# Seven-product tiles of an up product: four weight pieces, three interleaved tiles, other times for the weight sums

## The chip, the cores and the metric

One core of a Trainium2 chip runs one whole encoder layer. The metric is the device time of one execution in microseconds (us), as the median of several runs; lower is better. The engines are PE (TensorE, the matmuls), DVE (VectorE), ACT (ScalarE), POOL (GpSimd) and SP (SyncE, which here only issues DMAs). Each engine works through its own instructions in order and waits on semaphores for the others.

## The reference

The input is one sequence of 512 positions with 1024 features, float32. The layer has a mixing half (retention, and a gated unit that mixes over positions) and a feed-forward half. What the change touches is the first product of the feed-forward half:

```python
def _conv_gated_mlp(h, w_up, conv_w, conv_b, w_down):
    hid = h @ w_up                                   # (512, 1024) @ (1024, 5632)
    ...
    hid = lax.conv_general_dilated(                  # over 3 neighbouring positions, channel by channel
        ...) + conv_b
    a, b = jnp.split(hid, 2, axis=-1)
    return (jax.nn.gelu(a) * b) @ w_down             # (512, 2816) @ (2816, 1024)

# in reference()
h = _rmsnorm(x, g_pre_mix)
proj = h @ w_in                                      # q, k, v, g, u, sv and two gates
...
x = x + _rmsnorm(merged @ w_out, g_post_mix)
h2 = _rmsnorm(x, g_pre_ffn)
x = x + _rmsnorm(_conv_gated_mlp(h2, w_up, conv_w, conv_b, w_down), g_post_ffn)
```

## The kernel before

A float32 product is made as three matmuls of a faster type: each operand is split into a high and a low part, and hi·hi, hi·lo and lo·hi are added in PSUM. `split` makes the parts of a weight block: ACT copies it to `wf` or `wh` (the high part, by `copy`, L105), DVE subtracts that from the raw block (L163).

**Stages.** In the profile the projections and the retention lie up to about 215 us, u and the two gates from 215 to 400, the output projection, the norms and the first tiles of the up product up to about 480, the rest of the up product to about 650, the down product after that.

**The up product.** It makes 22 tiles of 128 channels of a and of b. Twelve of them, three in each of four groups (GROUPS, the first tile numbers 4, 8, 12, 16), are made with seven half-size products instead of eight (class `Pair`, after Strassen and Winograd); the fourth tile of a group is made whole, as two blocks of 24 matmuls of 128x512 (`f_block`). The three are called a, b and c below. A product of a Pair is twelve matmuls of 128x256. Its products, in the order in which one tile takes them, are M1 and M1' (`part1`, with the weight as it is), S1, S2, S3 (with sums of the activations and of the weights), and the two of `part3`, x4 and S4. M1 and S2, S3 and x4 gather in one PSUM bank: M1 is copied out by ACT first, then S2 is added to the bank and copied out again, and so on. So S2 waits for M1's copy. Where a tile's seven products lie between those of the others is written out by hand, in the loop over `i`.

**The weights of a Pair.** Blocks are fetched in the order of the list `units`, ahead of their use (`w_get`): SP issues the load into a raw buffer (`raw_tile`, four buffers), then the block is split. A seven-product tile has the unit u1 (the weight, 1024 columns), u2 (two sums, t12, 1024 columns), u3 (a third sum, 512) and u4 (a fourth sum and the rest of the weight, 1024).

**The weight sums.** The sums t12, t3 and t4 of a tile are not made by an engine but by DMAs from the weights in DRAM into DRAM: a copy (`sums_copy`, issued by ACT) and accumulating transfers (`sums_add`, issued by POOL, L131), seven for each tile. SUMS_AT says at which count of calls of `copy` each is issued, so it sets when they run. In the profiled execution count 67 falls at 133 us, 104 at 170, 140 at 213, 150 at 226, 285 at 396, 312 at 483 and 360 at 555.

**After the products.** `tile_done` convolves a finished tile (`conv`: steps on ACT L1321 and DVE L1324, L1328), applies gelu (ACT L1335), multiplies (DVE, `gp`, L1337) and, at the tiles of FORMS_AT, makes the forms of the activations for the down product (`down_forms`): sums `fs` and differences on DVE (L1363 to L1366), each high part `fh` by ACT's copy, and for the low part `fl` ACT writes −fh (L1346) and POOL issues an accumulating DMA that adds the source (L1347). `tc.issue_after(x)` holds what is within it back behind instruction x.

**Buffers.** `blk` gives blocks of 512 columns from one pool of 66 that many values share (c, gp, fs, fh, fl); who gets which is settled in the order of the program. The scheduler then orders the instructions of each engine by its own estimate of times.

Of the kernel before, what the change touches and what calls it, by code (L numbers as in the profile page):

```python
# [17 lines left out]
S = 512  # L18
# [24 lines left out]
).split()]  # L43
GROUPS = range(4, 20, 4)
SEVENS = [i + n for i in GROUPS for n in range(3)]
SUMS_AT = [a + k * (b - a) // n for a, b, n in ((29, 67, 28), (106, 140, 14), (150, 285, 14), (286, 300, 7), (312, 360, 21)) for k in range(n)]
FORMS_AT = (7, 9, 11, 13, 17, 19, 20, 21)

PRE, FFNG, LNG, LNB = 0, 8, 16, 24
# [6 lines left out]
def tile_block(ctx: ExitStack, tc, xT, x, wall, par, cs, wsp, bsp, gpost, gffn, out):  # L56
# [11 lines left out]
    def blk(dt=F32, n="blk", shape=(P, S)):  # L68
        return sb.tile(list(shape), dt, tag="blk", bufs=NBLK, name=nm(n))
# [34 lines left out]
    def copy(o, i):  # L104
        done = nc.scalar.activation(out=o, in_=i, func=AF.Copy)  # L105
        copies[0] += 1
        while sums_at and copies[0] >= sums_at[0]:
            sums_at.pop(0)
            sums_ops.pop(0)(done.ins)
        return done  # L110
# [35 lines left out]
    def two(t):  # L146
        return t.rearrange("p (n c) -> p n c", n=2)
# [13 lines left out]
    def split(hi, lo, src):  # L161
        copy(hi, src)
        low[0] = nc.vector.tensor_sub(lo, src, as32(hi)).ins  # L163
# [3 lines left out]
    RES1 = NW - 22 - 44  # L167
    RES0 = RES1 - RES_OUT
    FORMS = ("B11", "B21", "T1", "T2", "T3", "T4", "B22")
    units = []  # L170
    i = 0
    while i < NW:
        pair = [(f, i) for f in FORMS]
        if i == SV0:
            units += [(f, k) for f in ("s11", "sT1", "sT2") for k in range(2)]
            units += [(f, k) for k in range(2) for f in ("s22", "sT3")]
            units += [(f, k) for f in ("s21", "sT4") for k in range(2)]
            i = U0
        elif i == U0:
            us, gs = ([[(f, k + n * m) for f in FORMS] for n in range(KD // 2)] for k, m in ((U0, 2), (GATE0, 4)))  # L180
            ws = [("blk", GATE0 + 4 * (n // 2) + 2 + n % 2) for n in range(KD)]
            for what, n in MIDDLE:
                units += {"W": lambda: ws[n : n + 1], "U1": lambda: us[n][:4], "U2": lambda: us[n][4:],
                          "G1": lambda: gs[n][:4], "G2": lambda: gs[n][4:]}.get(what, list)()
            i = GATE0 + 2 * KD
        elif GATE0 <= i < GATE1:
            units += pair[:4] + [("blk", i + 2)] + pair[4:] + [("blk", i + 3)]
            i += 4
        elif i == UP0 + 2 * GROUPS[0]:
            for g in GROUPS:  # L190
                a, b, c = ([(f, g + n) for f in ("u1", "u2", "u3", "u4")] for n in range(3))
                w = [("blk", UP0 + 2 * (g + 3) + n) for n in range(2)]
                units += a[:2] + b[:2] + a[2:3] + w[:1] + a[3:] + b[2:3] + c[:2] + b[3:] + c[2:3] + w[1:] + c[3:]
            i = UP0 + 2 * (GROUPS[-1] + 4)
        elif i == DOWN0:
            for _ in range(2):
                pairs = [[("q", i + j), ("t", i + j)] for j in range(DP)]
                whole = [[("blk", i + DP)], [("blk", i + DP + 1)]]
                for u in pairs[:4] + whole[:1] + pairs[4:6] + whole[1:] + pairs[6:] if i == DOWN0 else pairs + whole:
                    units += u  # L200
                i += DP + WHOLE // 2
        else:
            units.append(("blk", i))
            i += 1
# [3 lines left out]
    def raw_tile():  # L208
        return sb.tile([P, 1024], F32, tag="raw", bufs=4, name=nm("raw"))
# [4 lines left out]
    def slot(n, at=0, w=1024):  # L214
        return sb.tile([P, 1088], F32R, tag="w4", bufs=9, name=nm(n))[:, at : at + w]
# [46 lines left out]
    def w_up(form, i):  # L262

        t12, t3, t4 = sums[SEVENS.index(i)]
        raw, i = raw_tile(), UP0 + 2 * i
        if form == "u3":
            raw = raw[:, :S]
            nc.sync.dma_start(raw, t3)
            w = slot("wf", 0, 1088)
            lo, hi = w[:, AT_64 : AT_64 + S], w[:, S + AT_192 : 2 * S + AT_192]  # L270
        else:
            if form == "u4":
                nc.sync.dma_start(raw[:, :S], t4)
                nc.sync.dma_start(raw[:, S:], wall[i + 1, :, S:])
            else:
                nc.sync.dma_start(raw, wall[i] if form == "u1" else t12)
            hi, lo = slot("wf", AT_192), slot("wf", AT_64)
        split(hi, lo, raw)
        return hi, lo

# [64 lines left out]
    kinds = {"b": lambda _, i: w_block(i), "u": w_up, "q": w_down, "t": w_down, "s": w_sv}  # L345

    def w_size(u):
        return 2 if u[0] in ("blk", "q", "t", "u1", "u2", "u4") or u[0][0] == "s" else 1

    def w_get(look=LOOK):  # L350

# [623 lines left out]
    class Pair:  # L975
# [39 lines left out]
        def part1(self):  # L1015

            c0, c1 = self.t

            def second():
                o = self.product(1, self.x(4, T0), True)  # L1020
                self.sum = v.tensor_add(two(c0[:, T0]), o, two(c0[:, T0])).ins

            o = self.product(0, self.x(0, T0), True)
            copy(two(c0[:, T0]), o)
            second()
            self.product(2, self.s("S1"), True)
            o = self.product(0, self.s("S2"), False)
            self.copied = copy(two(c1[:, T0]), o).ins
            if self.scale is not None:
                v.tensor_mul(c0[:, T0], c0[:, T0], self.scale[:, T0])  # L1030
# [9 lines left out]
        def part3(self):  # L1040
            c0, c1 = self.t
            o = self.product(0, self.x(4, T1), False, self.w[0])
            if self.scale is None:
                copy(two(c0[:, T1]), o)
            else:
                v.tensor_mul(two(c0[:, T1]), o, two(self.scale[:, T1]))
                if self.func:
                    nc.scalar.activation(out=c0, in_=c0, func=self.func)
            o = self.product(2, self.s("S4"), False, self.w[1])
            v.tensor_sub(two(c1[:, T0]), o, two(c1[:, T0]))  # L1050
            if self.scale is not None:
                v.tensor_mul(c1, c1, self.scale)
                if self.func:
                    nc.scalar.activation(out=c1, in_=c1, func=self.func)
# [264 lines left out]
    def conv(o, m):  # L1319
        c = tmp("cv")  # L1320
        nc.scalar.activation(  # L1321
            out=c, in_=o, func=AF.Identity, scale=col(CW + 3 * m + 1), bias=col(CB + m)
        )
        v.scalar_tensor_tensor(  # L1324
            out=c[:, 1:S], in0=o[:, 0 : S - 1], scalar=col(CW + 3 * m), in1=c[:, 1:S],
            op0=ALU.mult, op1=ALU.add,
        )
        v.scalar_tensor_tensor(  # L1328
            out=c[:, 0 : S - 1], in0=o[:, 1:S], scalar=col(CW + 3 * m + 2), in1=c[:, 0 : S - 1],
            op0=ALU.mult, op1=ALU.add,  # L1330
        )
        return c

    def gated(ca, cb):
        nc.scalar.activation(out=ca, in_=ca, func=AF.Gelu_apprx_tanh)  # L1335
        gp.append(blk(n="gp") if len(gp) < 2 * DP else (hi192, lo64)[len(gp) % 2]("gp", F32))
        v.tensor_mul(gp[-1], ca, cb)  # L1337
# [43 lines left out]
        dforms.append(forms_)  # L1381

    def tile_done(i, o):
        gated(*(conv(t, 2 * i + s_) for s_, t in enumerate(o)))
        if i in FORMS_AT:
            down_forms(len(dforms))

# [10 lines left out]
            split(h_, l_, s_)  # L1398
            h2forms[n] += [(h_[:, t], l_[:, t]) for t in (T0, T1)]

    def seven(alloc=tmp):
        p = Pair(None, lambda: alloc(n="c"), (h2h, h2l, h2forms))
        p.part1()
        return p

    i, waiting = 0, []
    while i < NF:
        if i in GROUPS:
            a = seven()
            with tc.issue_after(a.copied):  # L1410
                while waiting:
                    tile_done(*waiting.pop(0))
            b = seven(blk)
            a.part2()
            o = [f_block(h2h, h2l, KD)]
            a.part3()
            b.part2()
            c = seven(blk)
            with tc.issue_after(c.copied):
                tile_done(i, a.t)  # L1420
            b.part3()
            c.part2()
            with tc.issue_after(c.copied):
                tile_done(i + 1, b.t)
            o.append(f_block(h2h, h2l, KD, c.part3))
            waiting += [(i + 2, c.t), (i + 3, o)]
            i += 4
        else:
            o = []
            for e in (2 * i, 2 * i + 1):  # L1430
                o.append(early_o[e] if e < EARLY else f_block(h2h, h2l, KD))
                while waiting:
                    tile_done(*waiting.pop(0))
            tile_done(i, o)
            for k in {0: (0,), 1: (2,)}.get(i, ()):
                h2_forms(k)
            i += 1
# [319 lines left out]
```

## Time and profile before

| | |
|---|---|
| median of 3 runs (lowest, highest) | 792.87 us (792.85, 793.17) |
| the profiled execution | 793.08 us, of which the span is 791.3 |
| granted TensorE clock | 0.998 |
| PE busy | 774.7 us, 98% of the span |
| DVE, ACT, POOL busy | 630.4, 490.8, 145.6 us |
| HBM read and written | 125.94 and 29.36 MB |

The span runs from the first instruction to the last; 1.8 us of the time lie outside it. Busy times are read against the span. A line of the profile names a group by its line in the kernel, the engine, and output<-inputs by tile names; L105 and L163 are the helpers `copy` and `split`, so one reads those by their tiles (c<-ps is a copy out of PSUM, fh<-fs a form, wf<-raw a weight).

### The profile page before, as it was taken

The page shows a single profiled execution, that of the slowest core. Times are in us where ns is not written, and L with a number is a line of the kernel's source. Part 1 is how long each engine was busy: PE and PEld are TensorE (multiplying, and loading weights), DVE is VectorE, ACT ScalarE, POOL GpSimd, SP SyncE. Part 2 cuts the span into 40 slices and gives each one's busy share as a digit, 9 for nine tenths or more (in the row PEclk, how much of TensorE's full clock was granted, in tenths as well). Part 3 has the DMA queues.
Part 4 walks back from the last instruction along what each step waited for, and adds up shares of the span by engine and source line. Part 5 has one row for each costly group of instructions (what it writes and reads, how often), then busy time and mean ns, then how long its engine had stood idle before and what let it go on. Part 6 is the DMA issues. An engine that isn't in the chain of part 4 may idle for free. (4 is left out here: it accounts for less than half of the span.)

```text
span 791.3 us, 13995 instructions
## 1 busy us (share of the span) xinstructions
PE 774.7 (98%) x5283; PEld 722.2 (91%) x5283; DVE 630.4 (80%) x1057; ACT 490.8 (62%) x878; POOL 145.6 (18%) x180
## 2 busy tenths in 40 slices
PE   9999999999999999999999999999999999999996
PEld 8888998998999999899998898999889998999996
DVE  6477887889788997977764669778787979987887
ACT  7555468788475764744553676466778767854532
POOL 0040231232212201242230211011321102300001
PEclk9999999999999999999999999999999999999999
DMA  8796798467734443445469216797977764853344
GB/s 284 266 277 189 173 224 256 105 164 176 207 97 130 108 142 116 129 123 143 165 209 353 86 55 168 244 252 198 247 195 215 188 198 92 167 168 108 107 160 160
DMA packets 51827, 139.43 MB, mean 176 GB/s; under 512 B 6320, under 2 KB 8240, under 8 KB 51568
## 3 DMA queue, kind: packets, MB, share of 16 engines
q1 hardware_dynamic: 33120, 97.25, 37.0%
q0 software_dynamic: 13936, 27.53, 19.3%
q10 hardware_dynamic: 4704, 13.77, 5.2%
q8 instruction: 41, 0.67, 0.4%
q14 instruction: 26, 0.21, 0.1%
HBM read 125.94 MB, written 29.36 MB: 196 GB/s over the span
## 5 line engine op out<-in xcount | busy, mean ns | idle before, releaser
L105 ACT ACTIVATE wf<-raw 128x512 fp32r<-128x512 f32 (+1 forms) x132 | 97.0, 743 | 92.4 <-DMA raw<-wall 29.1
L999 PE MATMUL ps<-sh,wf 128*128 128x256 f32 x768 | 141.6, 277 | 5.2 <-ACT c L105 2.2
L163 DVE TENSOR_TENSOR wf<-raw,wf 128x512 fp32r<-128x512 f32 (+1 forms) x132 | 120.9, 923 | 29.2 <-ACT wf L105 28.6
L999 PEld LDWEIGHTS ps<-sh,wf 128*128 128x128 f32 x768 | 122.0, 192 | 8.5 <-ACT c L105 3.4
L163 DVE TENSOR_TENSOR wl<-raw,wh 128x1024 fp32r<-128x1024 f32 (+1 forms) x76 | 88.1, 1169 | 47.2 <-ACT wh L105 16.3
L999 PE MATMUL ps<-sl,wf 128*128 128x256 f32 x384 | 105.5, 275 | 0.0
L105 ACT ACTIVATE wh<-raw 128x1024 fp32r<-128x1024 f32 (+2 forms) x80 | 76.7, 970 | 30.9 <-DMA raw<-wall 19.7
L999 PEld LDWEIGHTS ps<-sl,wf 128*128 128x128 f32 x384 | 73.7, 192 | 0.2
L367 PE MATMUL ps<-h2l,wh 128*128 128x512 f32 (+1 forms) x192 | 66.3, 345 | 0.4 <-DVE h2l L1257 0.3
L366 PE MATMUL ps<-h2h,wh 128*128 128x512 f32 (+1 forms) x192 | 66.3, 345 | 0.0
L368 PE MATMUL ps<-h2h,wl 128*128 128x512 f32 (+1 forms) x192 | 66.1, 344 | 0.0
L1460 PE MATMUL ps<-dl,fh 128*128 128x256 f32 x216 | 59.5, 275 | 0.9 <-DVE dl L163 0.9
L1460 PE MATMUL ps<-dh,fh 128*128 128x256 f32 x216 | 59.4, 275 | 0.0
L1460 PE MATMUL ps<-dh,fl 128*128 128x256 f32 x216 | 59.4, 275 | 0.0
L999 PE MATMUL ps<-xh,wf 128*128 128x256 f32 x288 | 52.2, 275 | 0.8 <-ACT sig L105 0.8
L999 PE MATMUL ps<-h2h,wf 128*128 128x256 f32 x288 | 52.4, 275 | 0.0
L105 ACT ACTIVATE dh<-raw 128x768 fp32r<-128x768 f32 (+1 forms) x36 | 33.5, 947 | 26.4 <-DVE raw L295 18.8
L700 PE MATMUL ps<-wh,xh 128*128 128x512 f32 x128 | 48.6, 380 | 0.0
L701 PE MATMUL ps<-wl,xh 128*128 128x512 f32 x128 | 48.5, 379 | 0.0
L702 PE MATMUL ps<-wh,xl 128*128 128x512 f32 x128 | 48.4, 379 | 0.0
L999 PEld LDWEIGHTS ps<-xh,wf 128*128 128x128 f32 x288 | 45.6, 192 | 1.2 <-ACT sig L105 0.9
L999 PEld LDWEIGHTS ps<-h2h,wf 128*128 128x128 f32 x288 | 45.7, 192 | 0.5 <-ACT c L105 0.2
(345 smaller groups left out, 2223.1 us busy)
## 6 DMA issues: line engine op xcount, KB each, us to landing
raw<-wall SPq DMA_DIRECT2D x132, 512.0 KB, 4.5
x<-x SPq DMA_DIRECT2D x24, 256.0 KB, 5.9
sum<-wall ACTq DMA_DIRECT2D x12, 512.0 KB, 6.4
sum<-wall ACTq DMA_DIRECT2D x24, 256.0 KB, 6.0
sum<-wall POOLq DMA_DIRECT2D x24, 256.0 KB, 6.2
sum<-sum POOLq DMA_DIRECT2D x24, 256.0 KB, 6.2
raw<-sum SPq DMA_DIRECT2D x12, 512.0 KB, 6.2
raw<-sum SPq DMA_DIRECT2D x24, 256.0 KB, 3.6
```

The costliest lines, as they stand in the source:

```text
L105: done = nc.scalar.activation(out=o, in_=i, func=AF.Copy)
L163: low[0] = nc.vector.tensor_sub(lo, src, as32(hi)).ins
L366: nc.tensor.matmul(o, ah, bh, start=start, stop=False, skip_group_check=skip)
L367: nc.tensor.matmul(o, ah, bl, start=False, stop=False, skip_group_check=skip)
L368: pe_last[0] = nc.tensor.matmul(o, al, bh, start=False, stop=stop, skip_group_check=skip).ins
L700: nc.tensor.matmul(acc[t], xh[k][:, c], turns(wh[:, f]), start=k == 0, stop=False)
L701: nc.tensor.matmul(acc[t], xh[k][:, c], turns(wl[:, f]), start=False, stop=False)
L702: part_end[0] = nc.tensor.matmul(acc[t], xl[k][:, c], turns(wh[:, f]), start=False, stop=k == KD - 1)
L999: self.last = nc.tensor.matmul(o, w_[:, c], a_, start=first and k == n == 0, stop=k == 3 and n == 2, skip_group_check=True,)
L1460: nc.tensor.matmul(o, a_[:, c], turns(w_[:, f]), start=j == t == i == 0, stop=j == DP - 1 and i == 2 and n not in (M2, M3, M4), skip_group ...
```

## The change

A seven-product tile gets its weight in other pieces: uB (the weight, 1024 columns, a raw buffer), u1 and u2 (the two halves of t12) and u3, 512 columns each, in `ur` buffers that come from `blk`, and u4 as before. A group thus has 8 loads into raw buffers instead of 14, and 9 into `ur`, and one split more for each tile. `part1` ends after S1; S2 is a part of its own. The three tiles are interleaved in another way, and the end of c is put into the next group, behind the first products of its a. The result buffers of all three tiles now come from `blk`; those of a did not before. And the sums' times change: none is issued between count 140 and 312; 15 more come before it, 6 more after.

```diff
-SUMS_AT = [a + k * (b - a) // n for a, b, n in ((29, 67, 28), (106, 140, 14), (150, 285, 14), (286, 300, 7), (312, 360, 21)) for k in range(n)]
+SUMS_AT = [a + k * (b - a) // n for a, b, n in ((25, 67, 32), (68, 104, 10), (106, 140, 15), (312, 366, 27)) for k in range(n)]
...
-                a, b, c = ([(f, g + n) for f in ("u1", "u2", "u3", "u4")] for n in range(3))
+                a, b, c = ([(f, g + n) for f in ("uB", "u1", "u2", "u3", "u4")] for n in range(3))
                 w = [("blk", UP0 + 2 * (g + 3) + n) for n in range(2)]
-                units += a[:2] + b[:2] + a[2:3] + w[:1] + a[3:] + b[2:3] + c[:2] + b[3:] + c[2:3] + w[1:] + c[3:]
+                units += a[:2] + last + b[:2] + a[2:3] + b[2:3] + w[:1] + a[3:4] + b[3:4]
+                units += c[:2] + a[4:] + b[4:] + c[2:3] + w[1:] + c[3:4]
+                last = c[4:]
...
     def w_up(form, i):
...
+        if form in ("uB", "u4"):
+            raw = raw_tile()
...
+        else:
+            raw = blk(n="ur")
+            nc.sync.dma_start(raw, {"u1": t12[:, :S], "u2": t12[:, S:], "u3": t3}[form])
+            w = slot("wf", 0, 1088)
...
         if i in GROUPS:
             a = seven()
-            with tc.issue_after(a.copied):
-                while waiting:
-                    tile_done(*waiting.pop(0))
-            b = seven(blk)
+            while waiting:
+                waiting.pop(0)(a.first)
+            b = seven()
+            a.part_s2()
+            b.part_s2()
+            o = [f_block(h2h, h2l, KD)]
+            with tc.issue_after(b.copied):
+                o.append(conv(o[0], 2 * i + 6))
             a.part2()
-            o = [f_block(h2h, h2l, KD)]
+            b.part2()
+            c = seven()
             a.part3()
-            b.part2()
-            c = seven(blk)
-            with tc.issue_after(c.copied):
+            b.part3()
+            with tc.issue_after(b.ended):
                 tile_done(i, a.t)
-            b.part3()
-            c.part2()
+            c.part_s2()
             with tc.issue_after(c.copied):
                 tile_done(i + 1, b.t)
-            o.append(f_block(h2h, h2l, KD, c.part3))
-            waiting += [(i + 2, c.t), (i + 3, o)]
+            o.append(f_block(h2h, h2l, KD))
+            c.part2()
+
+            def rest(after, i=i, c=c, o=o):
+                with tc.issue_after(after):
+                    c.part3()
+                    tile_done(i + 2, c.t)
+                    tile_done(i + 3, [o[0], o[1], conv(o[2], 2 * i + 7)])
+
+            waiting.append(rest)
```

`a.first` is the copy of M1, `b.ended` that of x4. In the order that the scheduler gives PE, a group now runs: M1, M1', S1 of a; x4, S4 of the c before it; M1, M1', S1 of b; S2 of a; a whole block and S2 of b (in groups 2 and 3 the block first); S3 of a, of b; M1, M1', S1 of c; x4, S4 of a, of b; S2 of c; the second block; S3 of c.

The first place is ACT's queue in group 3, where the copy of b's M1 stands. In before, c_6684 with ps_6686 is the copy of tile b's M1, c_6572 with ps_6574 belongs to tile a, fh and fl are the down product's forms:

```order
L105 ACTIVATE fh_6669<-fs_6664 128x512 [waits DVE_49]
L105 ACTIVATE c_6572<-ps_6574 128x256 [waits PE_49]
L1346 ACTIVATE fl_6670<-fh_6669 128x512 [waits Activation_49]
L105 ACTIVATE fh_6674<-gp_5976 128x512
L105 ACTIVATE wf_6806<-raw_6803 128x1024 [waits DMAHW7_49,DMAHW6_49,PE_49]
L1346 ACTIVATE fl_6675<-fh_6674 128x512 [waits Activation_49]
L105 ACTIVATE fh_6679<-gp_5911 128x512 [waits DVE_49]
L1346 ACTIVATE fl_6680<-fh_6679 128x512 [waits Activation_49]
L105 ACTIVATE c_6684<-ps_6686 128x256 [waits DMASW3_49]
```

In the changed kernel the same forms; c_6703 with ps_6705 is the copy of tile b's M1, the two c that follow are the copies of S2 of a and of b:

```order
L1332 ACTIVATE cv_6673<-ps_6528,part 128x512
L105 ACTIVATE fa_6680<-gp_5942 128x256
L105 ACTIVATE fh_6688<-fs_6683 128x512 [waits DVE_49]
L1357 ACTIVATE fl_6689<-fh_6688 128x512 [waits DMASW0_49,Activation_49]
L105 ACTIVATE fh_6693<-gp_5974 128x512
L1357 ACTIVATE fl_6694<-fh_6693 128x512 [waits Activation_49]
L105 ACTIVATE fh_6698<-gp_5942 128x512 [waits DVE_49]
L1357 ACTIVATE fl_6699<-fh_6698 128x512 [waits Activation_49]
L105 ACTIVATE c_6703<-ps_6705 128x256 [waits DMASW5_49,DMASW4_49,PE_49]
L105 ACTIVATE c_6573<-ps_6574 128x256 [waits PE_49]
```

The copy of b's M1 stands behind all six forms in both; the weight split and the copy for tile a that lay among the forms have moved out of them.

DVE's queue of the changed kernel ahead of those forms begins when c_6336, of the tile c before, has had its S4 added (L1061):

```order
L1061 TENSOR_TENSOR c_6336<-ps_6339,c_6336 128x256 [waits PE_49]
L163 TENSOR_TENSOR wf_6555<-ur_6553,wf_6555 128x512 [waits DMAHW2_49,Activation_49]
L1335 SCALAR_TENSOR_TENSOR cv_6662<-c_6335,part,cv_6662 128x511 [waits Activation_49]
L163 TENSOR_TENSOR wf_6579<-ur_6577,wf_6579 128x512 [waits DMAHW3_49,Activation_49]
L163 TENSOR_TENSOR wf_6584<-ur_6582,wf_6584 128x512 [waits DMAHW4_49,Activation_49]
L1339 SCALAR_TENSOR_TENSOR cv_6662<-c_6335,part,cv_6662 128x511 [waits DVE_49]
L163 TENSOR_TENSOR wl_6628<-raw_6625,wh_6627 128x1024 [waits Activation_49]
L163 TENSOR_TENSOR wf_6633<-ur_6631,wf_6633 128x512 [waits DMAHW5_49,Activation_49]
```

Four more convolution steps, two gp and the sums for the forms follow these rows; the four splits of 512 columns now lie between the steps.

The second place is SP's queue of loads for group 4. Before, tile 16's first pieces (sum_0_90 is its t12) and tile 17's (sum_0_93) go to raw buffers:

```order
L276 DMA raw_6967<-sum_0_90 128x1024 [waits DMASW6_49,DMAHW0_49,DMASW2_49,DVE_49]
L276 DMA raw_7021<-wall 128x1024 [waits DMAHW1_49,DVE_49]
L276 DMA raw_7040<-sum_0_93 128x1024 [waits DMAHW2_49,DMASW5_49,DMAHW3_49,DMASW1_49,DVE_49]
L268 DMA raw_7089<-sum_1_91 128x512 [waits DMAHW4_49,DMASW0_49,DVE_49]
L221 DMA raw_7120<-wall 128x1024 [waits DMAHW5_49,DVE_49,Activation_49]
```

In the changed kernel:

```order
L273 DMA raw_7325<-sum_2_95 128x512 [waits DMAHW4_49,DMASW0_49,DMAHW7_49,DVE_49,Activation_49]
L274 DMA raw_7325<-wall 128x512
L280 DMA ur_7077<-sum_0_93 128x512 [waits DMASW5_49,Activation_49]
L280 DMA ur_7101<-sum_0_90 128x512 [waits DMASW2_49,DVE_49,Activation_49]
L280 DMA ur_7106<-sum_0_93 128x512 [waits DMASW4_49,DMAHW0_49,DMASW3_49,Activation_49]
L280 DMA ur_7155<-sum_1_91 128x512 [waits DMAHW6_49,DMAHW1_49,DVE_49]
L225 DMA raw_7370<-wall 128x1024 [waits DMAHW2_49,DVE_49]
```

ur_7101 (u2 of tile 16) has the buffer of `fs_7026`, and its load waits for the DMA of POOL that reads it (fl_7032<-fs_7026); ur_7106 (u2 of tile 17) waits in the same way for fl_7037<-gp_6136. The u4 load of tile 17 (raw_7325) now stands ahead of all of these.

More of the change, by code (lines that the diff above doesn't have):

```diff
@@ L169, in tile_block @@
     FORMS = ("B11", "B21", "T1", "T2", "T3", "T4", "B22")
-    units = []
+    units, last = [], []
     i = 0
@@ L190, in tile_block @@
             for g in GROUPS:
-                a, b, c = ([(f, g + n) for f in ("u1", "u2", "u3", "u4")] for n in range(3))
+                a, b, c = ([(f, g + n) for f in ("uB", "u1", "u2", "u3", "u4")] for n in range(3))
                 w = [("blk", UP0 + 2 * (g + 3) + n) for n in range(2)]
-                units += a[:2] + b[:2] + a[2:3] + w[:1] + a[3:] + b[2:3] + c[:2] + b[3:] + c[2:3] + w[1:] + c[3:]
+                units += a[:2] + last + b[:2] + a[2:3] + b[2:3] + w[:1] + a[3:4] + b[3:4]
+                units += c[:2] + a[4:] + b[4:] + c[2:3] + w[1:] + c[3:4]
+                last = c[4:]
             i = UP0 + 2 * (GROUPS[-1] + 4)
+            units += [("blk", i)] + last
+            i += 1
         elif i == DOWN0:
@@ L264, in w_up @@
         t12, t3, t4 = sums[SEVENS.index(i)]
[L265 to L271, printed above, removed]
+        i = UP0 + 2 * i
+        if form in ("uB", "u4"):
+            raw = raw_tile()
             if form == "u4":
@@ L275, in w_up @@
             else:
-                nc.sync.dma_start(raw, wall[i] if form == "u1" else t12)
+                nc.sync.dma_start(raw, wall[i])
             hi, lo = slot("wf", AT_192), slot("wf", AT_64)
+        else:
+            raw = blk(n="ur")
+            nc.sync.dma_start(raw, {"u1": t12[:, :S], "u2": t12[:, S:], "u3": t3}[form])
+            w = slot("wf", 0, 1088)
+            lo, hi = w[:, AT_64 : AT_64 + S], w[:, S + AT_192 : 2 * S + AT_192]
         split(hi, lo, raw)
@@ L347, in w_size @@
     def w_size(u):
-        return 2 if u[0] in ("blk", "q", "t", "u1", "u2", "u4") or u[0][0] == "s" else 1
+        return 2 if u[0] in ("blk", "q", "t", "uB", "u4") or u[0][0] == "s" else 1
     def w_get(look=LOOK):
@@ L1023, in part1, with part_s2 @@
             o = self.product(0, self.x(0, T0), True)
-            copy(two(c0[:, T0]), o)
+            self.first = copy(two(c0[:, T0]), o).ins
             second()
             self.product(2, self.s("S1"), True)
+            if self.h is xh:
+                self.part_s2()
+        def part_s2(self):
+            c0, c1 = self.t
             o = self.product(0, self.s("S2"), False)
@@ L1043, in part3 @@
             if self.scale is None:
-                copy(two(c0[:, T1]), o)
+                self.ended = copy(two(c0[:, T1]), o).ins
             else:
@@ L1383, in tile_done @@
     def tile_done(i, o):
-        gated(*(conv(t, 2 * i + s_) for s_, t in enumerate(o)))
+        if len(o) == 2:
+            o = [conv(t, 2 * i + n) for n, t in enumerate(o)]
+        gated(*o[-2:])
         if i in FORMS_AT:
@@ L1399, in h2_forms, with seven @@
             h2forms[n] += [(h_[:, t], l_[:, t]) for t in (T0, T1)]
-    def seven(alloc=tmp):
-        p = Pair(None, lambda: alloc(n="c"), (h2h, h2l, h2forms))
+    def seven():
+        p = Pair(None, lambda: blk(n="c"), (h2h, h2l, h2forms))
         p.part1()
@@ L1432, in tile_block @@
                 while waiting:
-                    tile_done(*waiting.pop(0))
+                    waiting.pop(0)(pe_last[0])
             tile_done(i, o)
```

## The prediction

> **What bounds the kernel now.** First the head of the page and the waits of PE over the whole span (engine and line, what it waited for, total us, times, longest):
>
> ```profile
> span 791.3 us, 13995 instructions
> PE 774.7 (98%) x5283; PEld 722.2 (91%) x5283; DVE 630.4 (80%) x1057; ACT 490.8 (62%) x878; POOL 145.6 (18%) x180
> ...
> PE ps L999 <- ACT sig L105: 2.8, 4, 0.9
> PE ps L999 <- ACT c L105: 2.2, 4, 0.9
> ...
> PE ps L999 <- DVE c L1036: 0.5, 1, 0.5
> ```
>
> TensorE sets the time: it is idle for 791.3 − 774.7 = 16.6 us in all, and the change leaves its matmuls as many as they were. So the change is worth what it does to PE's waits. Next the stretches, with PE, PEld, DVE, ACT and POOL busy, the granted clock, the share of the DMA engines and GB/s; the rows are the retention, u and the gates, and then two of the up product:
>
> ```profile
> 40.00:215.00 175.00, 175.00 (x977) 157.45 (x977) 140.24 (x244) 115.92 (x202) 45.55 (x65) 1.00 0.75 196
> 215.00:400.00 185.00, 181.74 (x1320) 171.68 (x1319) 155.22 (x245) 109.35 (x186) 42.27 (x33) 1.00 0.46 133
> ...
> 520.00:560.00 40.00, 39.81 (x307) 37.99 (x306) 31.76 (x48) 28.57 (x49) 10.61 (x13) 1.00 0.89 224
> 560.00:600.00 40.00, 37.61 (x285) 35.44 (x283) 33.32 (x51) 29.60 (x53) 6.97 (x8) 1.00 0.79 213
> ```
>
> PE never waits beside the retention, 3.3 us beside u and the gates, 2.7 us in the up product (the two rows of the waits for c), nearly all of it from 560 to 600. The clock is 1.00 throughout. The timeline of PE (start, duration) shows what a wait there is, and how long a piece of work is. Of eight such places the first is the row at 553.17, the last the row at 602.18:
>
> ```profile
> 553.17 0.38 PE L999 MATMUL ps<-sh,wf 128*128 128x256 f32 x1
> ...
> 588.55 0.38 PE L366 MATMUL ps<-h2h,wh 128*128 128x512 f32 x1
> ...
> 593.74 0.27 PE L999 MATMUL ps<-h2h,wf 128*128 128x256 f32 x1
> ...
> 596.41 0.28 PE L999 MATMUL ps<-h2h,wf 128*128 128x256 f32 x1
> ...
> 599.09 0.28 PE L999 MATMUL ps<-sh,wf 128*128 128x256 f32 x1
> 600.10 0.38 PE L999 MATMUL ps<-sh,wf 128*128 128x256 f32 x1 [0.74 <-ACT c L105]
> 600.32 0.28 PE L999 MATMUL ps<-sl,wf 128*128 128x256 f32 x1
> ...
> 602.18 0.38 PE L999 MATMUL ps<-sh,wf 128*128 128x256 f32 x1
> ```
>
> A whole F block (24 matmuls) takes 593.74 − 588.55 = 5.2 us; two products of twelve take 599.09 − 596.41 = 2.68, so one takes 1.34 and a matmul 0.112. From 599.09 to 600.32 two matmuls took 1.23, not 0.22: this wait cost 1.0 us where the idle column says 0.74. Read so, from start to start, the eight waits cost 4.8 us (0.24 at 553.17, the first, and 0.29 at 602.18, the last). ACT at that place:
>
> ```profile
> 595.99 0.62 ACT L1346 ACTIVATE fl<-fh 128x512 fp32r<-128x512 f32 x1
> 596.51 0.63 ACT L105 ACTIVATE fh<-gp 128x512 fp32r<-128x512 f32 x1
> 597.04 1.04 ACT L105 ACTIVATE wf<-raw 128x1024 fp32r<-128x1024 f32 x1
> 597.98 0.61 ACT L1346 ACTIVATE fl<-fh 128x512 fp32r<-128x512 f32 x1
> ...
> 599.68 0.37 ACT L105 ACTIVATE c<-ps 128x256 f32<-128x256 f32 x1
> 599.95 0.62 ACT L105 ACTIVATE wf<-raw 128x512 fp32r<-128x512 f32 x1
> 600.47 1.05 ACT L105 ACTIVATE wh<-raw 128x1024 fp32r<-128x1024 f32 x1
> ```
>
> The wait is for the copy of a tile's M1 out of PSUM (599.68). The copy had long been possible, but ACT works in order, and it stood behind the six instructions that make forms for the down product (fh, fl). Those wait for DVE's convolution chain. A transfer or a raw buffer is not what is late here.
>
> **The change, part by part.** *The work on PE* is the same; I cost it at nothing.
>
> *One load of 1024 columns becomes two of 512, so a tile has one split more.* From start to start ACT takes 0.52 for a split of 512 (599.95 to 600.47) and 0.94 for one of 1024 (597.04 to 597.98): 0.10 more per tile, 1.2 us over twelve tiles. DVE's starts stand here, and serve below:
>
> ```profile
> 588.82 0.69 DVE L1337 TENSOR_TENSOR gp<-cv,cv 128x512 f32<-128x512 f32 x1
> 589.42 0.75 DVE L1328 SCALAR_TENSOR_TENSOR cv<-ps,part,cv 128x511 f32<-128x511 f32 x1
> ...
> 590.74 0.69 DVE L163 TENSOR_TENSOR wf<-raw,wf 128x512 fp32r<-128x512 f32 x1
> 591.34 0.75 DVE L1328 SCALAR_TENSOR_TENSOR cv<-ps,part,cv 128x511 f32<-128x511 f32 x1
> 592.00 1.22 DVE L163 TENSOR_TENSOR wf<-raw,wf 128x1024 fp32r<-128x1024 f32 x1
> 593.13 0.69 DVE L1337 TENSOR_TENSOR gp<-cv,cv 128x512 f32<-128x512 f32 x1
> ...
> 594.06 0.43 DVE L1363 TENSOR_TENSOR fs<-gp,gp 128x256 f32<-128x256 f32 x1
> 594.40 0.43 DVE L1036 TENSOR_TENSOR c<-ps,c 128x256 f32<-128x256 f32 x1
> ```
>
> A convolution step takes 0.66 (591.34 to 592.00), gp 0.60 (588.82 to 589.42), a split of 512 0.60, of 1024 1.13, a 256-wide one 0.34; two splits of 512 cost 0.07 more than one of 1024. All this lies beside PE, since in each of those 40 us DVE is idle for 6.7 or more and ACT for over 10; it counts only where one of them is late, which is priced next.
>
> *The M1 copies.* Between a tile's M1 and its S2, which needs the copy, there now lie three to seven products, for b a block besides, where there were mostly two. That should remove the waits of before where the copy stands free in ACT's queue. It does not in groups 2 and 3, where b's copy is behind the forms burst of the group before. I follow group 3 from t = 0 at the end of group 2's second block. PE does c.S3, M1, M1', S1 of a, then x4 and S4 of c, then M1, M1', S1 of b and a.S2: ten products, 13.4; the block, 5.2; b.S2 is due at 18.6. DVE can start the convolution of c when c.S4 has been added, after six products: 8.0 + 0.3 = 8.4. In its queue then stand four splits of 512 (2.4), one of 1024 (1.1), six convolution steps (4.0), two gp (1.2) and five 256-wide ones (1.7): 18.8, the sum fs two of those earlier, at 18.1. ACT then makes six forms at 0.53 (596.51 to 597.04), 21.3, and the copy, 0.27: 21.6. PE waits 3.0, with the signal about 3.1. (The burst of before at this place had the wait of 1.0 at 600.10 as its result.) One split of 1024 less in that queue, or one more that is late, gives the ends 2 and 4.
>
> Group 2 in the same way: two splits of 512 and one of 1024 (2.3), six convolution steps (4.0) and two gp (1.2) from 8.4 on give 15.9, fs 0.7 later, 16.6. On ACT two wide forms (1.1), five narrow ones and the copy (six at 0.27, 1.6) follow: 19.3, against 18.6. That is 0.7; I take 1.3, since ACT's gelu, which both engines wait for, lies in that chain. Ends 0.5 and 3.
>
> *The ur buffers.* They come from the shared pool, and two of group 4 get the buffers that fs and a gp of the forms in group 3's tail just left; SP's load of tile 16's u2 so waits until the accumulating transfer fl<-fs, issued by POOL after ACT's fl, has landed. Times to landing: from 500 to 650 by kind (median), then of all accumulations of L1347 and of SP's 256 KB loads of a sum, L268 (minimum, median, maximum):
>
> ```profile
> fl<-fs POOLq DMA_DIRECT2D x4, 256.0 KB, 5.3
> fl<-gp POOLq DMA_DIRECT2D x4, 256.0 KB, 7.3
> ...
> DMA to landing us min/median/max: 2.7/5.8/11.8
> ...
> DMA to landing us min/median/max: 2.6/3.6/8.5
> ```
>
> With t = 0 at the end of group 3's second block, c.S3 ends at 1.3; ACT's copy in front of the forms can't be earlier, and DVE's chain (two tiles of convolutions from −7.2 on) gives fs at 3.4, so fl is written at 4.6. Landing, by the 5.3: 9.9. SP's issue and landing 0.3 + 3.6: 13.8. ACT's split 0.6: 14.4. a.S2 is due after nine products, at 12.1: a wait of 2.3. The next load, of b's u2, waits for fl<-gp in the same way, from 5.5: with 7.3 it is issued at 12.8 and split at 17.3, and the block's own split (1.0), for which PE waits next, stands behind it on ACT: 18.3, against 12.1 + 2.3 + 1.3 = 15.7, so 2.6 more; with L1347's median of 5.8 instead 1.1 more. I take 2.2, together 4.5. With the smallest landings, 2.7 and 2.6, nothing is late: 0. With the longest load, 8.5, it is 4.5 + 4.9 = 9.4. Behind the waiting load on SP stand the loads of u3 and the next block, so I let nothing of it be won back.
>
> The Trainium skill (DMA: Bandwidth & Descriptors, Anatomy of one DMA — SWDGE (gpsimd) path) fits such a transfer as 2.0 us plus its bytes over 436 GB/s, an estimate of 2.6 us for these 256 KB. The trace has 5.3 and 7.3 for the two here, so I go by the trace; by the page the wait for u2 would not exist, which is the second rival.
>
> *Smaller places.* SP now has the u4 loads ahead of b's ur loads, and each c starts just as its load comes: 0.3 in each of three groups, 0.3 in group 1: 1.2 (0 to 2.5).
>
> *The weight sums.* From 226 to 412 us ACT and POOL lose these issues:
>
> ```profile
> sum<-wall ACTq DMA_DIRECT2D x7, 256.0 KB, 5.6
> sum<-sum POOLq DMA_DIRECT2D x6, 256.0 KB, 4.3
> sum<-wall POOLq DMA_DIRECT2D x4, 256.0 KB, 4.3
> sum<-wall ACTq DMA_DIRECT2D x2, 512.0 KB, 5.8
> ```
>
> PE's waits there are for ACT's copies of sig (2.8 us above), and the DMA engines' share there is 0.46. Nothing shows them to come from a transfer; gain between 0 and 2.8, I take 0. Fifteen of the transfers go ahead of 215 us, where PE never waits and the DMA share is 0.75: 0, at most 1. Six go beside the first up groups (share 0.89): 0, at most the third rival.
>
> **Sum.** Waits in the up product 1.3 + 3.1 + 4.5 + 1.2 = 10.1 instead of 4.8: +5.3. Against the profiled execution (793.08, which is 0.21 above the median of 792.87) that is 798.4, as a median 798.2. With all ends together the waits are 2.5 to 18.9; they are not likely to fall together, so I take 6 to 14: 794 to 802.
>
> **Rivals.** *It works as drawn (faster).* If DVE's chain in group 3 ends before about 15 (its splits done ahead, in PE's ten products) and the ur loads of group 4 are early, every copy is made in its new, longer cover. For it: no S2 is now nearer than three products to its M1. Against: the queue on DVE, counted above. The waits fall from 4.8 to about 1: 789.1.
>
> *The waits only move (the same).* With the accumulation and the load at their quickest, u2 is split at 4.6 + 2.7 + 0.3 + 2.6 + 0.6 = 10.8, before 12.1. Group 4 then costs nothing, and 1.3 + 3.1 + 1.2 = 5.6 stands against the 4.8 of before: 793.7. For it: both durations are in the trace, and the DMA share is already lower from 560 than before it. Against: 5.3 and 7.3 are medians of this stage.
>
> *The transfers are the bound beside the first groups (much slower).* Six sums more at a share of 0.89, and loads that go halfway to their longest, some 2.4 us later than the median: the three tiles of groups 1 and 2 then wait about 1 us each more, 798.2 + 6 = 804. Against: PE lost 0.19 us in 520 to 560.
>
> **Numbers.** Forecast 0.47, as drawn 0.25, only moved 0.18, transfers 0.10. Less than 0.2% (1.6 us) is about what a measurement of this kernel can't tell from no change. Faster gets the first rival and little else, 0.25; the same the second, and a part of the forecast's lower edge, 0.20; slower the rest, 0.55. The range is 789.0 to 802.0: it leaves out half of the first rival and most of the last; the forecast's own is 794 to 802.
>
> **What would show it.** In the profile after, PE at 480 to 650 waits for ACT c once in group 2 (about 1 us) and once in group 3 (about 3), each time at S2 behind a block, with fh and fl rows just ahead of the copy on ACT; in group 4 it waits for ACT wf or wh, and SP at the line of the ur loads waits for a transfer fl<-fs. If SP shows no such wait, group 4 is wrong; if fs is made over 3 us before b.S2 is due, group 3 is. u and the gates should read the same, 2.8 for sig. The forecast is wrong as a whole if PE's waits in the up product stay under 4 us.

## The result, and the profile after

The changed kernel takes 807.94 us (median of five runs, 805.22 to 809.32) against 793.17 (792.85 to 794.38) for the one before: slower by a factor of 1.0174, 95% interval 1.0148 to 1.0200. The profiled execution took 808.35 us, its span is 806.5, that of before 791.3. Slower was forecast, but 798.2, and the range ended at 802. The head of the page after, and PE's waits:

```profile
span 806.5 us, 14015 instructions
PE 779.0 (97%) x5283; PEld 726.8 (90%) x5283; DVE 632.1 (78%) x1069; ACT 494.3 (61%) x890; POOL 144.1 (18%) x180
...
PE ps L1004 <- ACT c L105: 11.0, 3, 4.5
PE ps L1004 <- ACT wf L105: 3.9, 3, 2.3
PE ps L373 <- DVE wl L163: 1.4, 2, 0.9
```

The matmuls are the same 5283, yet PE is busy for 4.3 us more; and there is no wait for sig and none for xn any more. The stretches of before again (PE, PEld, DVE, ACT, POOL busy, granted clock, DMA share, GB/s), with 400 to 480 and 600 to 640 added:

```profile
40.00:215.00 175.00, 174.45 (x968) 156.36 (x967) 139.44 (x241) 116.63 (x202) 50.69 (x72) 1.00 0.86 221
215.00:400.00 185.00, 184.79 (x1350) 175.56 (x1349) 156.66 (x248) 110.60 (x186) 35.54 (x25) 1.00 0.36 117
400.00:480.00 80.00, 80.00 (x487) 73.24 (x486) 55.19 (x106) 51.12 (x129) 14.43 (x22) 1.00 0.40 140
520.00:560.00 40.00, 33.48 (x227) 31.50 (x226) 28.98 (x44) 26.38 (x49) 11.56 (x14) 0.91 0.84 195
560.00:600.00 40.00, 33.95 (x250) 31.57 (x249) 30.26 (x51) 26.71 (x50) 7.71 (x10) 0.98 0.71 202
600.00:640.00 40.00, 37.03 (x278) 35.41 (x277) 27.00 (x42) 25.23 (x43) 3.18 (x4) 0.94 0.61 166
```

```profile
400.00:480.00 80.00, 78.27 (x479) 70.81 (x478) 49.96 (x98) 47.17 (x125) 16.95 (x25) 1.00 0.54 173
```

Two opposite things happened. From 215 to 480 PE now waits for next to nothing, where before it waited for 3.3 us beside u and the gates and 1.7 from 400 to 480 (the row of before for that stretch stands here alone). In the up product it is idle for 6.5, 6.1 and 3.0 us in three stretches of 40, and the granted clock is 0.91 and 0.94 in two of them. Measured from start to start over all rows of PE, and against the usual distance of 0.112 us for 256 columns and 0.216 for 512, the change gained 4.3 us from 215 to 400 (4.9 to 0.6) and 2.9 from 400 to 480 (2.8 to nothing), lost 1.1 from 40 to 215, 20.7 from 480 to 660 (4.5 to 25.2) and 0.5 behind that: 15.1 of the 15.2 us between the spans.

The worst place is b.S2 of group 2, the one at 599.70 in group 3 is its twin (4.67 us). PE there:

```profile
546.21 0.38 PE L373 MATMUL ps<-h2h,wl 128*128 128x512 f32 x1
551.03 0.58 PE L1004 MATMUL ps<-sh,wf 128*128 128x256 f32 x1 [4.44 <-ACT c L105]
551.40 0.42 PE L1004 MATMUL ps<-sl,wf 128*128 128x256 f32 x1
551.61 0.63 PE L1004 MATMUL ps<-sh,wf 128*128 128x256 f32 x2
552.04 0.42 PE L1004 MATMUL ps<-sl,wf 128*128 128x256 f32 x1
```

From 546.21 to 551.03 is 4.82, 4.6 more than the usual 0.216. Behind the wait the matmuls start 0.21 apart, not 0.112, until 557.2: half clock, some 2.7 us more (the granted clock is 0.50 from 551 to 557). ACT ahead of it:

```profile
532.39 0.41 ACT L105 ACTIVATE fa<-gp 128x256 fp32r<-128x256 f32 x1
536.91 0.63 ACT L105 ACTIVATE wf<-ur 128x512 fp32r<-128x512 f32 x1 [4.11 <-DMA ur<-sum]
...
543.84 0.64 ACT L1346 ACTIVATE cv<-cv 128x512 f32<-128x512 f32 x1 [0.77 <-DVE cv L1339]
547.89 0.63 ACT L105 ACTIVATE fh<-fs 128x512 fp32r<-128x512 f32 x1 [3.41 <-DVE fs L1375]
...
550.61 0.36 ACT L105 ACTIVATE c<-ps 128x256 f32<-128x256 f32 x1
```

The copy that PE waits for (550.61) does stand behind the forms, as forecast. But the forms are late themselves: 4.1 us went at 536.91, where ACT waited for a `ur` load. The issues of SP say why that was late, with two rows of SP's waits behind them:

```profile
527.57 0.33 SPq L273 DMA_DIRECT2D raw<-sum  x1
...
530.38 0.33 SPq L273 DMA_DIRECT2D raw<-sum  x1
530.75 0.43 SPq L274 DMA_DIRECT2D raw<-wall  x1
531.28 1.80 SPq L280 DMA_DIRECT2D ur<-sum  x4
...
SPq L273 <- DVE wf L163: 27.4, 9, 5.6
...
SPq L280 <- DMA fl<-fs: 5.6, 1, 5.6
```

Four ur loads wait behind two u4 loads (L273), and those wait until DVE has read a raw buffer. The last row is the wait that was forecast for group 4.

### The profile page after: what moved, and what is told of

It reads as the page before. It is cut to its first block, busy times and chain, and to the rows that moved or that the text cites. A ratio compares the mean times of both kernels' runs of the same rounds, so it can differ in the third digit from the quotient of the medians.

```text
span 806.5 us, 14015 instructions
## 1 busy us (share of the span) xinstructions
PE 779.0 (97%) x5283; PEld 726.8 (90%) x5283; DVE 632.1 (78%) x1069; ACT 494.3 (61%) x890; POOL 144.1 (18%) x180
## 5 line engine op out<-in xcount | busy, mean ns | idle before, releaser
L1004 PE MATMUL ps<-sh,wf 128*128 128x256 f32 x768 | 147.0, 283 | 14.5 <-ACT c L105 11.0
L1004 PEld LDWEIGHTS ps<-sh,wf 128*128 128x128 f32 x768 | 126.6, 198 | 17.4 <-ACT c L105 12.2
L163 DVE TENSOR_TENSOR wl<-raw,wh 128x1024 fp32r<-128x1024 f32 (+1 forms) x76 | 86.4, 1147 | 38.5 <-ACT wh L105 11.5
L105 ACT ACTIVATE wf<-raw 128x512 fp32r<-128x512 f32 (+1 forms) x108 | 76.8, 721 | 56.3 <-PE ps L372 19.6
L163 DVE TENSOR_TENSOR wf<-raw,wf 128x512 fp32r<-128x512 f32 (+1 forms) x108 | 98.4, 920 | 13.6 <-ACT wf L105 13.2
L1004 PE MATMUL ps<-sl,wf 128*128 128x256 f32 x384 | 108.1, 282 | 0.0
L1004 PEld LDWEIGHTS ps<-sl,wf 128*128 128x128 f32 x384 | 76.2, 199 | 0.3
```

The costliest lines, as they stand in the source:

```text
L1004: self.last = nc.tensor.matmul(o, w_[:, c], a_, start=first and k == n == 0, stop=k == 3 and n == 2, skip_group_check=True,)
```

## The experiments

**The two halves of the change apart.** The first kernel is the one before with the new table alone; the second the changed one with the old table:

```diff
 # the kernel before
-SUMS_AT = [... ((29, 67, 28), (106, 140, 14), (150, 285, 14), (286, 300, 7), (312, 360, 21)) ...]
+SUMS_AT = [... ((25, 67, 32), (68, 104, 10), (106, 140, 15), (312, 366, 27)) ...]
```

> The kernel before, with only the new times of the weight sums. Sums theory: the 6.6 us that PE gained ahead of the up product (waits from 220 to 460: 4.9 + 2.5 before, 0.7 after) come from the sums' times alone, and the 20 us lost in the up product come from the tiles' new order: 786 to 788. Rival, the gain comes from the new order of the scheduler or the sums beside the up product cost the loss: 793 or slower. Forecast's own term (sums worth nothing): 793.

It took 788.31 us, 0.9932 of before (0.9916 to 0.9949): the sums' times alone are a gain of about 5 us, as the sums theory had it (0.3 above its range). The waits of ACT for a weight load from 215 to 400 tell what it was, first in before and then in this kernel:

```profile
ACT wf L105 <- DMA raw<-wall: 25.7, 12, 4.9
```

```profile
ACT wf L105 <- DMA raw<-wall: 10.9, 11, 2.0
```

ACT, and PE behind it, waited for loads that shared the DMA engines with the sums: the loads that SP issued at 292.90 and 294.97 in before landed 8.1 and 7.1 us later, the same two (291.08 and 293.57) in this kernel 4.8 and 3.6. PE's own list named sig, a copy that stood behind the late split in ACT's queue.

> The changed kernel with the old times of the weight sums, so the tiles' new pieces and order alone. Sums theory: the gain ahead of the up product is lost, the waits in it stay: 813 to 816. Rival, six more sums beside the up product are what makes loads late there: the up product gets its waits back to about 10, 800 to 804. Forecast's own (sums nothing): 808.

803.67 us, 1.0132 (1.0117 to 1.0148). The rival's time (800 to 804) is met, but not its waits of about 10; the other two missed. PE has its waits at the gates and the norms back (from start to start 3.5 and 3.2 us), but loses only 14.8 in the up product, not 25.2. With the old times of the sums, the scheduler puts the four ur loads of group 2 ahead of the second of the two u4 loads (530.81 against 535.25), not behind it, and ACT's wait of 4.1 is this:

```profile
535.79 0.63 ACT L105 ACTIVATE wf<-ur 128x512 fp32r<-128x512 f32 x1 [0.31 <-DMA ur<-sum]
```

**The seven sums and the fourteen.** Only the fourteen sums beside u and the gates are moved, in the kernel before:

```diff
-SUMS_AT = [... ((29, 67, 28), (106, 140, 14), (150, 285, 14), (286, 300, 7), (312, 360, 21)) ...]
+SUMS_AT = [... ((25, 67, 32), (68, 104, 10), (106, 140, 14), (286, 300, 7), (312, 360, 21)) ...]
```

> The kernel before; of the weight sums' times only the fourteen between counts 150 and 285 (beside u and the gates) are moved ahead of them, the seven at 286 to 300 and those beside the up product stay. If the sums slow the weight loads beside which they run: u and the gates' 4.9 us of waits fall to about 0.7, the norms' 2.5 (437 to 456) stay, the retention gives 1 back: 790 (789 to 791). Rival, the gain of the sums alone came from the norms or the up product: 792 to 793.

791.71 us, 0.9991 (0.9972 to 1.0009), so the time alone shows nothing. The trace does: PE's waits at the gates (first row, 3.1 in before) are nearly gone, those at the norms (second row, 1.4 in before) grew, and from start to start they are 3.8 against 2.8.

```profile
PE ps L999 <- ACT u L105: 0.3, 1, 0.3
...
PE ps L1251 <- DVE xn L1236: 2.4, 3, 1.4
```

So the gain of the sums alone needs the seven at 286 to 300 moved as well. Why the norms wait longer here than in before stays open.

**Loads, forms and buffers.** Three edits of the changed kernel, one for each cause that could hold b.S2 or group 4:

```diff
 # loads: SP issues all loads of w_up in the order of the program
+    up_load = [None]
+
+    def w_load(o, i):
+        with tc.issue_after(up_load[0]) if up_load[0] else ExitStack():
+            up_load[0] = nc.sync.dma_start(o, i).ins
 ...
-                nc.sync.dma_start(raw[:, :S], t4)
+                w_load(raw[:, :S], t4)
 # forms: those of a group's whole tile not in rest(), but behind b's S2 of the next group
             b.part_s2()
+            while held:
+                held.pop()
+                with tc.issue_after(b.copied):
+                    down_forms(len(dforms))
 # pool: the six buffers of the convolution's values
-            raw = blk(n="ur")
+            raw = tmp("ur")
```

| kernel | us | of before (95%) |
|---|---|---|
| the change | 807.94 | 1.0174 (1.0148 to 1.0200) |
| + forms | 807.72 | 1.0178 (1.0163 to 1.0193) |
| + pool | 802.72 | 1.0125 (1.0098 to 1.0152) |
| + loads | 800.33 | 1.0085 (1.0066 to 1.0105) |
| + loads, forms | 792.56 | 0.9993 (0.9981 to 1.0006) |
| + loads, pool | 788.51 | 0.9944 (0.9927 to 0.9960) |
| + loads, forms, pool | 784.39 | 0.9883 (0.9856 to 0.9911) |

> The changed kernel; the forms of a group's whole tile are made behind the copy of b's S2 in the next group, not ahead of the copy of b's M1. Forms theory: the waits at b.S2 of groups 2 and 3 (4.6 and 4.7) and the stretch of half clock behind each (2.7 and 2.3) go: 808 - 13 = 795 (793 to 798). Loads theory (what is late is u1 and u2 themselves): PE then waits for the split instead, 804 to 808.

The forms theory failed here in its number: 0.2 us. The time is that of the loads theory. Yet the waits at b.S2 of groups 2 and 3 are gone. In group 2 a wait of 3.9 took their place a few us later, for a copy that stands behind a split whose ur load is late; waits of 1.8, 1.2 and 1.6 follow, and from 612 to 660 PE loses 9.6 us instead of 5.7. PE at the wait of 3.9, and then ACT:

```profile
562.08 0.38 PE L1004 MATMUL ps<-h2h,wf 128*128 128x256 f32 x1 [3.72 <-ACT c L105]
```

```profile
561.13 0.63 ACT L105 ACTIVATE wf<-ur 128x512 fp32r<-128x512 f32 x1 [4.42 <-DMA ur<-sum]
561.66 0.37 ACT L105 ACTIVATE c<-ps 128x256 f32<-128x256 f32 x1
```

> The changed kernel; SP issues the loads of the seven-product tiles in the order of their use, so that the ur loads no longer stand behind the next tiles' u4 loads, which wait for a raw buffer. Loads theory: ACT's waits for ur of 4.1 and 2.1 go, the convolution and the forms come that much earlier; group 2's wait falls from 4.6 to about 1 and its half clock goes (-6), group 3's to about 2.5 and the small waits at 585 and 590 go (-4): 797 to 800. Forms theory alone, loads not late: 806 to 808.

As the loads theory had it (its range ended 0.3 lower), 7.6 us less. From start to start the waits at 527, 585 and 590 (2.25, 1.0 and 1.0) are gone, group 2's is 1.7 instead of 4.6 with no half clock behind it. Group 3's stays at 4.8, where about 2.5 was expected, so loads are not what holds that one. By groups, with half clock and new small waits, PE loses 2.3 us less than in the change in group 1, 5.1 in group 2 and 1.5 in group 3, and 1.4 more in group 4. PE from 480 to 660:

```profile
PE ps L1010 <- ACT c L105: 7.3, 3, 4.6
PE ps L1010 <- ACT wf L105: 3.5, 3, 2.4
```

> The changed kernel with both edits: the tiles' loads in the order of their use, and the forms of a group's whole tile behind the copy of b's S2. Forms theory, whose wait could not show while the loads were late: against loads alone (800.3) the waits at b.S2 of groups 2 and 3 (1.7 and 4.8) and the half clock behind the second (2.8) go: 791 (790 to 793). Rival, whatever stands behind the forms waits in its turn, as it did with the forms moved alone: 797 to 800.

The forms theory held, 1.6 us above its number: with the loads in order the same edit that was worth 0.2 us is worth 7.8. What is left in 480 to 660 is nearly all group 4's wait, with the releaser that was forecast (PE's wait, then SP's):

```profile
PE ps L1010 <- ACT wf L105: 3.8, 1, 3.8
...
SPq L270 <- DMA fl<-fs: 6.7, 1, 6.7
```

> As the last (loads and forms), and the ur buffers come from the six buffers that the convolution's temporary values use, not from the shared pool, so that no load of group 4 waits for an accumulation (fl<-fs). Buffer theory: group 4's waits (2.6 + 0.4 + 0.3 + 0.5 + 0.4, half clock 0.9, 1.3 at c.M1) mostly go: 4 to 5 us under the last kernel. Rival, the loads now wait for the convolution's buffers: the same or slower than the last.

8.2 us less than the last: more than the 4 to 5 expected, since that wait of 4.0 had grown and half clock followed it. This kernel is faster than both. All that PE waits for from 480 to 660 is

```profile
PE ps L1010 <- ACT c L105: 2.0, 3, 1.2
PE ps L1010 <- DVE c L1053: 0.6, 1, 0.6
```

> The changed kernel with one edit: the ur buffers from the convolution's six buffers, not from the shared pool; loads and forms as they are. If each of the three causes has its own waits: group 4's (2.5 + 0.4 + 0.3 + 0.7 + 1.3 and 0.4 of half clock, 5.6 us) go, 802 (800 to 804). The scheduler now also puts the ur loads of b ahead of its u4 load, so if that order alone was most of the loads' part: 797 to 800. Rival, it hides behind the others as the forms alone did: 806 to 808.

802.72 us, the number of the first theory, but not its reason: group 4 does not get better. From 612 to 660 PE loses 7.8 us, and 5.7 in the change. The waits for tile a's and b's pieces are gone there, but one of 4.0 is left, for a copy behind a split that waits for ur (ACT idle for 2.44); that load stands on SP behind a block's load that waited 8.2 us for a raw buffer. What was won lies ahead of it: the wait at 527 is gone, group 2 loses 6.8 us instead of 7.6 and group 3 3.8 instead of 9.7 (the waits at b.S2 are 1.5 and 1.9). With these buffers SP issues three of the four ur loads ahead of the second u4 load, so the gain is rather that of the order, as the second theory had it.

> Loads in order and the ur buffers from the convolution's six, the forms where the change has them. Forms theory: group 2's and 3's waits at b.S2 (1.7 and 4.8, and 2.8 of half clock) stay and group 4's go: 800.3 - 6 = 794 (792 to 796), so that the forms make the last 8 to 10 us to the 784.4 of all three. Rival, early buffers also let the convolution end earlier and the copy wait less: 788 or under.

788.51 us: nearer to the rival (788 or under). The forms make only the last 4.1 us, not 8 to 10; the waits at b.S2 are 2.2 and 1.9 with the forms ahead of the copy.

**The sums under the ordered loads.** The kernel of loads and forms with the table of the seven-and-fourteen test (six sums fewer beside the up product, seven at the norms):

> Loads and forms as in e5, with the sums' times of the kernel with the gates free: seven transfers at 286 to 300 and six fewer beside the up product. If six more sums beside the up product are what delays ur loads even when they are issued in order: faster in 500 to 560 by 2, slower at the norms by 2.5: the same as e5 within 1.5 us. If they only disturbed the order of the loads: 2 to 2.5 us slower than e5.

798.35 us, 1.0061 (1.0037 to 1.0086), 5.8 slower than the same with the new table: more than either theory said. From 480 to 660 PE loses 9.8 us, and 10.5 with the new table; from 215 to 480 it loses 6.0 instead of 0.3, of which the norms are the most (4.4; why they wait longer here than in before stays open, as above):

```profile
PE ps L1268 <- DVE xn L1253: 3.1, 3, 2.0
```

So six sums more beside the up product cost under 1 us once the loads are in order and the forms moved. The 10.4 us that they cost the changed kernel there (14.8 with the old table, 25.2 with the new) came, by these runs, mostly through the order that the scheduler chose.

## Why the prediction was wrong

*The steps that failed.* The forecast read the order of SP's loads and priced it at 1.2 us; it cost 7.6, of which 2.7 are half clock. It had no term for the half clock behind a long wait, which cost 5.0 in all. And it put the sums' times at nothing, which gained 7.2 ahead of the up product and so hid a part of the other two.

*The direction, and three places.* Slower was right, and each of the three waits that were priced is there with the releaser named: a copy behind fh and fl at b.S2 of groups 2 and 3, and SP's wait for fl<-fs ahead of group 4. That u and the gates would read the same, 2.8 for sig, was wrong: there is no wait for sig.

*The weight sums: "I take 0".* They gained 4.3 us at the gates and 2.9 at the norms, more than the upper end of 2.8 for the gates; the norms had no term. The step took PE's list for the cause and said that nothing shows a transfer; the row of ACT's waits with 25.7 us for raw<-wall shows it. The 1.1 us lost in the retention are the end that was given.

*The smaller places: 1.2.* Of the terms for the up product this is the one that failed most. The u4 loads stood ahead of b's ur loads in the order that the forecast read, and it took 0.3 a group for that. The order cost 7.6 us by the run that undoes it: 2.25 in group 1, 2.0 at 585 and 590, and in group 2 the 2.9 by which its wait then falls and the 2.7 of half clock behind it; new waits of 0.7 at two places and 1.4 more in group 4 go off that again.

*The M1 copies: 1.3 and 3.1.* Measured 4.6 and 4.7. With the loads in order group 2's is 1.7, so the working was nearly right for loads that come in time. Group 3's is 4.8 there too, 1.7 above: in that run DVE's first split comes at 575.23, 9.1 us after the block's end and not 8.4, sums that need each other stand 0.45 apart and not 0.34, and ACT's six forms take 3.56 and not 3.2 (585.49 to 589.05).

*The ur buffers: 4.5.* Measured 2.5 + 0.4 at a.S2, 0.3 + 0.7 in the block and 1.3 at c: 5.2. The total was nearly right by errors that cancel. The accumulation was quick, issued at 628.25 and followed by SP's load at 631.65, so 3.4 where 5.3 was taken; but with the block's end at 622.24 that is an issue at 6.0 and not 4.6. And a second row of the same pool was not seen: ACT's copy of a's M1, ahead of the split, itself waited 5.0 us for an accumulation out of the buffer that it was to write (u2 itself landed at 635.93, so the two held PE about equally long):

```profile
635.81 0.38 ACT L105 ACTIVATE c<-ps 128x256 f32<-128x256 f32 x1 [5.03 <-DMA fl<-gp]
636.09 0.62 ACT L105 ACTIVATE wf<-ur 128x512 fp32r<-128x512 f32 x1
```

The wait of 1.3 at c is for a ur load too, but that one waited for a convolution step (cv). With the other pool ACT waits for no accumulation from 590 to 650 in any of the three runs, so that edit frees the copy as well. Its worth depends on what else is late: 8.2 us behind loads and forms, 11.8 behind the loads; the 5.2 of the pool alone were not won in group 4.

*What had no term: the clock.* After both waits of 4.6 and 4.7 PE ran at half clock, some 2.7 and 2.3 us together 5.0. In before no wait was over 1.1 us, and the clock was 1.00 in every stretch up to 760.

*The rivals.* The first (it works as drawn) named its conditions, the convolution ending early and the ur loads early. No run made the convolution end that early; where the loads are early and the forms are out of the copy's way instead, the waits in 480 to 660 fell to 3.3 us, and with the sums' gain that is 784.4. The third had the loads late in groups 1 and 2, but by contention; with loads and forms put right, six sums fewer win less than 1 us. The second had the transfers of group 4 quick, which the accumulation was; that did not help, since it was issued later.

In the sum: 4.6 + 4.7 + 5.2 for the three priced places (8.9 forecast), 4.3 for the smaller ones (1.2), 5.0 for the clock and about 1.4 in single small gaps make 25.2 instead of 10.1; less 7.2 gained ahead of them, plus 1.1 and 0.5.

## What to carry to other kernels

When PE's list of waits names a copy or an activation, read what the engine that makes it waits for: here ACT's 25.7 us for loads stood behind PE's 2.8 for sig. A queue that issues loads in order is to be read like an engine, load by load, with what each waits for and who is behind it; a small change of times elsewhere can reorder it. Causes that follow one another hide each other: one edit was worth 0.2 us alone and 7.8 after another, so undo them together before one is dismissed.

## What was not expected of the hardware

A wait of PE costs more than its length once it is long. In all the runs here, every wait of 3.9 to 4.8 us (nine of them) was followed by 11 to 27 matmuls at twice the usual distance, 1.2 to 2.7 us. Of those between 1.9 and 2.6, two of 2.2 us were followed by 17 such matmuls (1.7 us) and two of 2.6 us by eight or nine, some of 512 columns (1.4 us); the others, three of 2.2 to 2.5 among them, by none to three. Shorter waits that stood alone were followed by none to two, but with the pool alone waits of 1.6, 0.9 and 1.5 within 5 us had 24 such matmuls among and behind them (2.4 us, granted clock 0.50 from 547.2 to 554). The Trainium skill (TensorE: Matmul & The Clock Gate, Part 1: The HAM clock gate) says that the clock goes to one half after an idle window of about 3.4 us. The waits of 3.9 and more agree; the runs also show half clock after 2.2 and 2.6, which are shorter than that, and why some of these waits had it and others not stays open.
